# A hybrid decoder block on one core: four seven-product pairs in the embedding gate, differences stored later and written as one operation, attention steps in another order

## The chip, the cores and the metric

The kernel runs on one core of a Trainium2 chip. The metric is device time in microseconds of one execution; less is better. Times here are medians of runs, and the profile is of one execution of its own.

## The reference

One decoder layer on x of 256 tokens by 2048 channels, in float32. All matmuls below are with weights read from memory once.

```python
proj = x @ w_in                       # splits: gq gk gv gr glr fq fk fv ff ma mb
o    = gla_chunked(q, k, v, log_a)    # 4 heads, chunks of 64, then RMS norm and silu(gr)
y_gla = o @ w_branch_gla
of   = fox_attention(fq, fk, fv, log_f)   # 8 heads, softmax over 256, blocks of 128
y_fox = of @ w_branch_fox
x = layer_norm(ALPHA*x + (sigmoid(ma)*y_gla + sigmoid(mb)*y_fox) @ w_out)
g = causal_dwconv(x @ w_gate, conv_w, conv_b)     # width 3, 5632 channels
x = layer_norm(ALPHA*x + (gelu(g) * (x @ w_up)) @ w_down)
x = x + sigmoid(x @ w_ple_gate) * (p @ w_ple_proj)
```

## The kernel before

Weights arrive in units of 1 MB (`wu[u]`, 128 partitions by 2048). Each value is split in two parts, `hi` (rounded copy, made by ScalarE) and `lo` (the rest, made by VectorE, line 254), so that the product keeps its accuracy; TensorE multiplies hi by all columns and lo by those of the activations' high part. The plain route is `prep(u)`: SyncE loads two `raw` tiles, ACT copies them to `hi{u}_0`, `hi{u}_1`, DVE subtracts to `lo{u}_0`, `lo{u}_1`. `unit()` prepares three units ahead. There are five raw buffers and six of hi and of lo.

Stages follow one another: fox projections, attention and GLA; branch projections; out projection; layer norm; `gate_up` with 88 units (136 to 223: for n = 0 to 43 a gate unit `psg{n}` and an up unit `psu{n}`, so `psg40` is unit 216); the down projection; the embedding gate (`pg`).

A unit of gate_up is 16 matmuls of 512 columns (hi) and 16 of 256 (lo), in pairs; every 14th unit (`TURN`) has another order: six pairs, then the other lo's, then the other hi's. When PE ends it, ACT copies half to `tmp`, DVE adds the other half (`gp` or `up`, line 363), POOL copies two columns for the conv, DVE does the conv on `yc`, ACT the gelu, and DVE multiplies by `up`; the result goes to a tile hC, of which there are eleven, each for four n. For some pairs of n DVE also forms `sums` and `hs`, stored by POOL to `sd`.

Some pairs of K tiles in the later stages are done by seven products of 2x2 blocks instead of eight: 21 matmuls of 512 columns instead of 24. They need sums of activations (`s_sums`, `g_sums`) and differences of weight blocks. For the pairs listed in a table ending in `_T` the differences are made early: `park_gen` loads the unit into a `td` tile (SyncE, line 191), DVE makes four differences in place (line 172), POOL stores the tile to memory (line 185), and `prep_s` loads it again when its stage comes. In gate_up the generator is advanced by `pull(1, parks)`, once an n: one n loads, the next n parks. Tiles `td`, hC (the first ten) and the four tiles `x1T` of activations share one pool of 15 buffers of 8 KB a partition, "S8".

The order of ACT, DVE, POOL and mostly PE is set by a planner from the program's dependences and its own costs; SyncE's queue keeps program order, and each engine runs its queue in order. So a load that waits for a buffer holds up all loads behind it. `fox_gen` gives out the three steps of each attention head (logits, turn, values) between other matmuls.

Of the kernel before, what the change touches and what calls it, by code (L numbers as in the profile page):

```python
# [14 lines left out]
ALU = mybir.AluOpType  # L15
# [4 lines left out]
P = 128  # L20
# [52 lines left out]
WO_T = ((1, 2, 3, 4, 5), (1, 3, 5))  # L73
DN_T = ((3, 6, 9, 12, 15, 18), (3, 6, 9, 12, 15))
PG_ORDER = (tuple(range(8)), tuple(range(8)))
PG_S = ((), (2, 3, 4))
PG_T = ((), (2, 3, 4))
AFF1 = ((0, 2, 3), (0, 2))
AFF2 = ((0, 2), (0, 2))
LN_ORDER = (1, 0, 3, 2)  # L80
# [7 lines left out]
def tile_block(ctx: ExitStack, tc: tile.TileContext, wu, wfv, wpp, xT_in, x_in, pT_in, wlr,  # L88
               chan, gnorm, lng, ident_in, mask_in, cmask_in, out):
    nc = tc.nc  # L90
# [77 lines left out]
        return rhi.tile([P, 1088], F32R, tag="hi", name=f"hi{name}")[:, o:o + 1024]  # L168

    def differences(r0, r1, h, pinned=False):  # L170
        b12, b11, b22, b21 = r0[:, 0:512], r0[:, 512:1024], r1[:, 0:512], r1[:, 512:1024]
        sub = lambda o, a, b: nc.vector.tensor_tensor(o, a, b, ALU.subtract)  # L172
        if h == 0:
            i = sub(b11, b12, b11)
            if pinned:
                tc.keep_in_program_order(i)
            sub(b12, b12, b22)
        else:
            sub(b22, b22, b11)
            sub(b21, b21, b22)  # L180

    def park(w, i):
        for h in range(2):
# [14 lines left out]
    def prep_s(u):  # L198


        r0, r1 = [ring.tile([P, 1024], F32, tag="raw", bufs=5, name=f"raw{u}_{h}")
                  for h in range(2)]
        b12, b11, b22, b21 = r0[:, 0:512], r0[:, 512:1024], r1[:, 0:512], r1[:, 512:1024]
        rt = (r0, r1)
        if u in parked:
            nc.sync.dma_start(b11, wu[u, :, 512:1024])
            nc.sync.dma_start(r1, wu[u, :, 1024:2048])
            w = s8([P, 2048], name=f"td{u}")
            nc.sync.dma_start(w, td[parked[u]])
            rt = (w[:, 0:1024], w[:, 1024:2048])  # L210
        else:
            for h, r in enumerate((r0, r1)):
                nc.sync.dma_start(r, wu[u, :, h * 1024:(h + 1) * 1024])
        if dn0 <= u < dn0 + NF:
            nh = (u - dn0) // (NF // 2)
            pair = DN_ORDER[nh][(u - dn0) % (NF // 2)]
            i = DN_S[0].index(pair)
            if i % 2 == 0:
                two = s8([P, 8, 256], F32R, name=f"hS{nh}_{pair}")
                nc.sync.dma_start(two.bitcast(F32), sd[i // 2].rearrange(  # L220
                    "p (i n) -> p i n", i=8))
                hS[nh, pair], hS[nh, DN_S[0][i + 1]] = two[:, 0:4], two[:, 4:8]

        def split(src, name, e=slice(0, 1024)):
            hi = hi_tile(u, f"{u}_{name}")[:, e]
            lo = lo_tile(u, f"{u}_{name}")[:, e]
            copy(hi, src)
            nc.vector.tensor_tensor(lo, src, hi.bitcast(F32), ALU.subtract)  # L228
            return [(hi[:, o:o + 512], lo[:, o:o + 512]) for o in range(0, src.shape[1], 512)]

        x11, = split(b11, "b11", slice(512, 1024))
        x22, x21 = split(r1, "b2")
        if u not in parked:
            differences(r0, r1, 0)
        t3, t1_ = split(rt[0], "t13")
        if u not in parked:
            differences(r0, r1, 1)
        t2_, t4 = split(rt[1], "t24")
        ready[u] = [x11, x21, x22, t1_, t3, t2_, t4]
# [245 lines left out]
    for u in range(8):  # L485
        hi, lo = fvu[u]
        for j in range(2):
            kt = 2 * u + j
            a = xT[kt // 4][:, kt % 4, :]
# [6 lines left out]
            for t, i, c in seq:  # L496
                o, n = fch[c]
# [35 lines left out]
    for t in range(2):  # L533
        for c, (o, n) in enumerate(fch):
            n = min(n, 1024 - o)
# [75 lines left out]
    def fox_gen():  # L611


        lgs, sts, ptss = {}, {}, {}
        halves = ((256, 128), (0, 256))

        def logits(h):
            pl = mxtile(f"pl{h}")
            q, k = [fqk[h // 4][:, h % 4, i] for i in range(2)]
            for t, (o, n) in enumerate(halves):  # L620
                nc.tensor.matmul(pl[:, o:o + n], lhsT=q[:, t * P:t * P + P], rhs=k[:, 0:n],
                                 start=True, stop=True)
            lg = lgs[h] = t2("lg")[:, 0:384]
            for t, (o, n) in enumerate(halves):
                nc.vector.scalar_tensor_tensor(lg[:, o:o + n], pl[:, o:o + n],
                                               ct[:, t * FH + h:t * FH + h + 1],
                                               ncb[:, h * 256:h * 256 + n], ALU.add, ALU.add)
            nc.vector.tensor_tensor(lg[:, P:384], lg[:, P:384], cmask, ALU.add)
            st = sts[h] = sm.tile([P, 8], F32, tag="fst", name="fst")
            nc.vector.tensor_reduce(st[:, 0:1], lg[:, 256:384], AX.X, ALU.max, negate=True)  # L630
            nc.vector.tensor_reduce(st[:, 1:2], lg[:, 0:256], AX.X, ALU.max, negate=True)

        def softmax(h):
            lg, st = lgs[h], sts.pop(h)
            for t, (o, n) in enumerate(halves):
                nc.scalar.activation(lg[:, o:o + n], lg[:, o:o + n], AF.Exp,
                                     bias=st[:, t:t + 1], scale=1.0,
                                     accum_out=st[:, 2 + t:3 + t])
            nc.vector.reciprocal(st[:, 4:6], st[:, 2:4])
            for t, (o, n) in enumerate(halves):  # L640
                nc.vector.tensor_scalar(lg[:, o:o + n], lg[:, o:o + n], st[:, 4 + t:5 + t],
                                        None, ALU.mult)

        def turn(h):
            lg = lgs.pop(h)
            pt = mxtile(f"pt{h}")
            for i, d in enumerate((1, 2, 0)):
                nc.tensor.transpose(pt[:, d * P:d * P + P], lg[:, i * P:i * P + P], ident)
            pts = ptss[h] = t2("pts")[:, 0:384]
            copy(pts, pt[:, 0:384])  # L650

        def values(h):
            pts = ptss.pop(h)
            po = mmtile(f"po{h}")
            nc.tensor.matmul(po[:, 0:256], lhsT=fv[:, 0, h * P:h * P + P], rhs=pts[:, 0:256],
                             start=True, stop=False)
            nc.tensor.matmul(po[:, 128:256], lhsT=fv[:, 1, h * P:h * P + P],
                             rhs=pts[:, 256:384], start=False, stop=True)
            dst = ofT[h // 4][:, h % 4, :]
            copy(dst[:, 0:256], po[:, 0:256])  # L660
            nc.vector.tensor_tensor(dst[:, 256:512], po[:, 0:256],
                                    dst[:, 0:256].bitcast(F32), ALU.subtract)

        for i in range(FH + 2):
            for f, h in ((values, i - 2), (turn, i - 1), (logits, i)):
                if 0 <= h < FH:
                    f(h)
            yield
            if i < FH:
                softmax(i)  # L670
            yield
# [7 lines left out]
    for n in range(16):  # L679
        h, j = n // 2, n % 2  # L680
# [115 lines left out]
    for n in range(16):  # L796
        nm, dst, sc = (("q", gq, 1.0 / 16.0), ("k", gk, 1.0))[n // 2 % 2]
        h, c = n // 4, n % 2
# [274 lines left out]
    for nh in range(2):  # L1073
        def ev_r(t, c, ps, nh=nh):
# [3 lines left out]
            if 2 * nh + c == 0:  # L1078
# [3 lines left out]
               residual=False)  # L1082
# [71 lines left out]
    for n in range(PSM1, 32):  # L1154
        if n in (26, 28):
            i = n // 2 - 13
# [290 lines left out]
    for n in range(NF):  # L1447
# [18 lines left out]
        u = t1("up")  # L1466
# [4 lines left out]
        if pair in DN_S[0]:  # L1471
            if j == 0:
                yp = t2("yp").rearrange("p (k t) -> p k t", t=S)
            h = yp[:, j, :]
        else:
            h = y
# [4 lines left out]
        if pair in DN_S[0] and j == 1:  # L1481
            v = s_sums(yp)
            for i in range(2):
# [5 lines left out]
                o = k % 2 * 1024 + 512 * i  # L1489
                nc.gpsimd.dma_start(sd[k // 2, :, o:o + 512],  # L1490
                                    w.rearrange("p i n -> p (i n)").bitcast(F32))
        if n >= 4:
            pull(1)
        if n >= 4:
            pull(1, parks)


# [135 lines left out]
    def g_sums(pairs):  # L1633
        two = s8([P, 8, 256], F32R, name=f"gS{pairs[0]}")
        for i, pair in enumerate(pairs):
            o = two[:, 4 * i:4 * i + 4]
            a = x2T[pair // 2][:, pair % 2 * 2:pair % 2 * 2 + 2, :].bitcast(F32)
            y = t2("gy").rearrange("p (k t) -> p k t", t=S)
            nc.vector.tensor_tensor(y, a[:, :, 0:256], a[:, :, 256:512], ALU.add)
            v = s_sums(y)  # L1640
            copy(o[:, :, 0:P], v)
            nc.vector.tensor_tensor(o[:, :, P:256], v, o[:, :, 0:P].bitcast(F32), ALU.subtract)
            gS_[pair] = o
# [25 lines left out]

    def mid4():  # L1670
        mid3()
        g_sums(PG_S[1][:2])

    x_half("pg0", x2T, 16, lambda t, c, ps: put(ps, 0, t, c), pulls=2,
           begin=begin2, mid=(mid4, 4))

    s_half("pg", 1, PG_ORDER[1], PG_S[1], g_cl, g_st, lambda t, g: zg[:, t, g - 2, :], ev_g,
           3, {0: lambda: g_sums(PG_S[1][2:])}, residual=False, fine=pre_g)
    assert n_used[0] == NU, (n_used[0], NU)


# [23 lines left out]
def _sst(w, orders, ssets):  # L1705


    out = []
    for nh, (order, sset) in enumerate(zip(orders, ssets)):
        for n in order:  # L1710
            b = [[w[(2 * n + j) * P:(2 * n + j + 1) * P,
                    nh * 1024 + c * 512:nh * 1024 + c * 512 + 512] for c in range(2)]
                 for j in range(2)]
            out.append(np.concatenate([b[0][1], b[0][0], b[1][1], b[1][0]] if n in sset
                                      else b[0] + b[1], 1))
    return np.stack(out)

# [67 lines left out]
```

## Time and profile before

| | |
|---|---|
| median of 3 runs | 1638.0 us (1636.72 to 1638.08) |
| profiled execution | 1637.74 us; its span 1635.9 us |
| TensorE clock granted in it | 1.0 |
| PE busy | 1629.3 us |
| DVE, ACT, POOL busy | 1356.9, 909.5, 91.2 us |
| moved by DMA | 477.81 MB, 292 GB/s |

The span is what the profile covers; 1.8 us of the execution lie around it. Busy time of PE is that of overlapping matmuls; how long a matmul holds PE is read from the starts of the next ones, or from counts in a stretch of time. DMA times are from issue to landing.

### The profile page before, as it was taken

To read this page: it belongs to the slowest core of one execution; us is meant where nothing else is said; L and a number is where in the kernel's file an instruction comes from. 1 tells how busy PE (TensorE), PEld (TensorE's weight loads), DVE (VectorE), ACT (ScalarE), POOL (GpSimd) and SP (SyncE) were. 2 spreads that over 40 slices of the span, in tenths; PEclk is the share of its full clock that TensorE was granted. 3 is DMA by queue.
4 is the path that set the end of the run, shared out by engine and by line. 5 is a ranking of instruction groups with operands and counts; after the bars stand their busy time and mean duration, and the time that the engine had idled before them with its cause. 6 is when DMAs were issued, how large, how long until landed. Compare 5 with 4: busy or idle time off the path is not lost.

```text
span 1635.9 us, 23491 instructions
## 1 busy us (share of the span) xinstructions
PE 1629.3 (100%) x8422; PEld 1396.6 (85%) x8422; DVE 1356.9 (83%) x1964; ACT 909.5 (56%) x1277; POOL 91.2 (6%) x244
## 2 busy tenths in 40 slices
PE   9999999999999999999999999999999999999998
PEld 9988888888888888888898888888888888888887
DVE  7698899788989867878987888888887788988787
ACT  6655555456666653446574455555455456566554
POOL 0000000000000000000010111110111000000000
PEclk9999999999999999999999999999999999999999
DMA  8799899878888758889856898888776679899574
GB/s 325 283 370 345 292 390 353 293 262 299 308 322 326 253 189 320 304 317 393 299 181 198 321 347 322 292 310 312 282 252 221 204 273 339 307 355 344 166 260 156
DMA packets 114838, 477.81 MB, mean 292 GB/s; under 512 B 13032, under 2 KB 14320, under 8 KB 95136
## 3 DMA queue, kind: packets, MB, share of 16 engines
q1 hardware_dynamic: 105216, 417.57, 71.9%
q0 software_dynamic: 9504, 58.73, 9.0%
q8 instruction: 66, 1.08, 0.3%
q14 instruction: 52, 0.43, 0.1%
HBM read 417.53 MB, written 58.73 MB: 291 GB/s over the span
## 4 chain that ended last, share of the span: by engine, by line
PE 96%; DVE 2%; DMA 1%; ACT 1%; issue 0%; POOL 0%; SPq 0%; ACTq 0%; DVEq 0%; POOLq 0%
PE psm L1006 11%; PE dn L868 10%; PE psu L319 9%; PE psg L319 8%; PE psa L1006 5%; PE psu L324 4%; PE psg L324 4%; PE dn_p L868 4%; PE wo L868 3%; PE gr L868 3%; PE gv L868 3%; PE pg L380 3%; PE psb L1006 3%; PE fv L499 2%; PE gr_p L868 2%; PE gv_p L868 2%
## 5 line engine op out<-in xcount | busy, mean ns | idle before, releaser
L254 DVE TENSOR_TENSOR lo<-raw,hi 128x1024 fp32r<-128x1024 f32 x456 | 551.9, 1222 | 135.7 <-ACT hi L130 134.6
L130 ACT ACTIVATE hi<-raw 128x1024 fp32r<-128x1024 f32 x456 | 476.9, 1057 | 299.0 <-DMA raw<-in_wu_dram 68.4
L319 PE MATMUL psg<-x1T,hi 128*128 128x512 f32 x672 | 231.2, 390 | 0.0
L319 PE MATMUL psu<-x1T,hi 128*128 128x512 f32 x688 | 230.2, 390 | 0.0
L324 PE MATMUL psg<-x1T,lo 128*128 128x256 f32 x672 | 186.2, 277 | 0.6 <-DVE lo L254 0.6
L324 PE MATMUL psu<-x1T,lo 128*128 128x256 f32 x688 | 180.5, 277 | 0.0
L1006 PE MATMUL psm<-hi,xT 128*128 128x512 f32 x512 | 163.1, 393 | 0.0
L319 PEld LDWEIGHTS psu<-x1T,hi 128*128 128x128 f32 x688 | 128.7, 188 | 26.7
L319 PEld LDWEIGHTS psg<-x1T,hi 128*128 128x128 f32 x672 | 126.2, 188 | 26.4
L130 ACT ACTIVATE hi_b<-raw 128x512 fp32r<-128x512 f32 x112 | 93.1, 841 | 68.3 <-DMA raw<-in_wu_dram 16.4
L324 PEld LDWEIGHTS psg<-x1T,lo 128*128 128x128 f32 x672 | 126.1, 188 | 0.9 <-DVE lo L254 0.9
L324 PEld LDWEIGHTS psu<-x1T,lo 128*128 128x128 f32 x688 | 125.3, 188 | 0.6
L172 DVE TENSOR_TENSOR td<-td 128x512 f32<-128x512 f32 x172 | 118.3, 688 | 0.9
L228 DVE TENSOR_TENSOR lo_b<-raw,hi_b 128x512 fp32r<-128x512 f32 x112 | 105.3, 955 | 16.5 <-ACT hi_b L130 16.2
L1006 PEld LDWEIGHTS psm<-hi,xT 128*128 128x128 f32 x512 | 96.2, 188 | 19.6
L228 DVE TENSOR_TENSOR lo_t<-td,hi_t 128x1024 fp32r<-128x1024 f32 x86 | 101.8, 1222 | 12.5 <-ACT hi_t L130 11.7
L130 ACT ACTIVATE hi_t<-td 128x1024 fp32r<-128x1024 f32 x86 | 88.1, 1053 | 31.3 <-DMA td<-td 20.2
L1006 PE MATMUL psm<-lo,xT 128*128 128x512 f32 x256 | 99.9, 390 | 0.0
L868 PE MATMUL dn<-hi,hC 128*128 128x512 f32 x352 | 97.9, 390 | 0.0
L1006 PE MATMUL psa<-hi,oT 128*128 128x512 f32 x256 | 81.3, 392 | 0.0
L868 PEld LDWEIGHTS dn<-hi,hC 128*128 128x128 f32 x352 | 66.0, 188 | 13.6
L1006 PEld LDWEIGHTS psa<-hi,oT 128*128 128x128 f32 x256 | 48.1, 188 | 9.9
(414 smaller groups left out, 3129.4 us busy)
## 6 DMA issues: line engine op xcount, KB each, us to landing
raw<-in_wu_dram SPq DMA_DIRECT2D x525, 512.0 KB, 6.3
td<-in_wu_dram SPq DMA_DIRECT2D x43, 1024.0 KB, 8.7
td<-td POOLq DMA_DIRECT2D x43, 1024.0 KB, 6.7
td<-td SPq DMA_DIRECT2D x43, 1024.0 KB, 8.0
hS<-sd SPq DMA_DIRECT2D x11, 1024.0 KB, 8.9
raw<-in_wu_dram SPq DMA_DIRECT2D x43, 256.0 KB, 7.6
fvraw<-in_wfv_dram SPq DMA_DIRECT2D x13, 524.0 KB, 6.7
sd<-hs POOLq DMA_DIRECT2D x24, 256.0 KB, 5.8
```

Source lines behind the costliest of these rows:

```text
L130: return nc.scalar.activation(o, i, AF.Copy, bias=0.0, scale=scale)
L172: sub = lambda o, a, b: nc.vector.tensor_tensor(o, a, b, ALU.subtract)
L228: nc.vector.tensor_tensor(lo, src, hi.bitcast(F32), ALU.subtract)
L254: i = nc.vector.tensor_tensor(lo, raw, hi.bitcast(F32), ALU.subtract)
L319: nc.tensor.matmul(ps, lhsT=hi[i // 8][:, i % 8 * P:i % 8 * P + P], rhs=act[kts[i] // 4][:, kts[i] % 4, :], start=first and i == 0, stop=l ...
L324: nc.tensor.matmul(ps[:, 256:512], lhsT=lo[i // 8][:, i % 8 * P:i % 8 * P + P], rhs=act[kts[i] // 4][:, kts[i] % 4, 0:256], start=False, s ...
L380: nc.tensor.matmul(bs[j][:, 0:m], lhsT=x, rhs=v[:, o:o + m], start=first and i == 0, stop=last and i == 2)
L499: nc.tensor.matmul(fbk[t][c][:, 0:n], lhsT=x, rhs=w[:, o:o + n], start=kt == 0 and i == 0, stop=kt == 15 and i == 2)
L868: nc.tensor.matmul(ps[:, e], lhsT=x, rhs=w, start=k == 1, stop=k == total.get(id(ps), 3 * ns))
L1006: nc.tensor.matmul(ps[t], lhsT=x, rhs=v, start=first and i == 0 and j == 0, stop=last and i == 3 and j == 2)
```

## The change

Four edits. The gate's second half treats pairs 1 to 4 by seven products instead of 2 to 4, all parked (44 parked units instead of 43), and forms the sums of both couples in the middle of the first half. In a parked tile the first two differences become one operation of 128x1024, with block b12 read twice; for this the host writes the first two blocks of such a unit in the other order. In the attention the steps of one turn go turn, logits, values instead of values, turn, logits. In gate_up the generator of parked units is advanced from n = 10 instead of n = 4.

```diff
-PG_S = ((), (2, 3, 4))
-PG_T = ((), (2, 3, 4))
+PG_S = ((), (1, 2, 3, 4))
+PG_T = ((), (1, 2, 3, 4))
...
     def differences(r0, r1, h, pinned=False):
...
+            two = r0.rearrange("p (i n) -> p i n", i=2)
+            if r0.tensor is r1.tensor:
+                four = bass.AP(tensor=r0.tensor, offset=r0.offset,
+                               ap=[r0.ap[0], [1024, 2], [1, 512]])
+                i = nc.vector.tensor_tensor(two, two[:, 1:2].broadcast_to([P, 2, 512]), four,
+                                            ALU.subtract)
...
-            for f, h in ((values, i - 2), (turn, i - 1), (logits, i)):
+            for f, h in ((turn, i - 1), (logits, i), (values, i - 2)):
...
-        if n >= 4:
+        if n >= 10:
             pull(1, parks)
...
     def mid4():
         mid3()
-        g_sums(PG_S[1][:2])
+        for i in (0, 2):
+            g_sums(PG_S[1][i:i + 2])
...
-           3, {0: lambda: g_sums(PG_S[1][2:])}, residual=False, fine=pre_g)
+           3, {}, residual=False, fine=pre_g)
...
-            out.append(np.concatenate([b[0][1], b[0][0], b[1][1], b[1][0]] if n in sset
+            out.append(np.concatenate([b[0][0], b[0][1], b[1][1], b[1][0]] if n in sset
```

How the change moves instructions late in gate_up. First SyncE's queue at the loads of units 215 to 217, before; a `raw` has its unit's number.

```order
L250 DMA raw214_1_12310<-in_wu_dram 128x1024
L250 DMA raw215_0_12361<-in_wu_dram 128x1024
L250 DMA raw215_1_12367<-in_wu_dram 128x1024
L250 DMA raw216_0_12413<-in_wu_dram 128x1024
L250 DMA raw216_1_12419<-in_wu_dram 128x1024
L250 DMA raw217_0_12470<-in_wu_dram 128x1024
```

SyncE at the same place now:

```order
L256 DMA raw214_1_12267<-in_wu_dram 128x1024
L256 DMA raw215_0_12318<-in_wu_dram 128x1024
L256 DMA raw215_1_12324<-in_wu_dram 128x1024
L197 DMA td43_12370<-in_wu_dram 128x2048
L256 DMA raw216_0_12372<-in_wu_dram 128x1024
L256 DMA raw216_1_12378<-in_wu_dram 128x1024
L256 DMA raw217_0_12429<-in_wu_dram 128x1024
```

The load of the last parked tile, td43, stands ahead of unit 216's raw loads; before, no parked tile is loaded this late.

VectorE around lo216_0, before; `psg38` is unit 212, `psu38` 213, `psu39` 215, and the `up` or `gp` line is the first DVE step after PE has ended that unit.

```order
L254 TENSOR_TENSOR lo215_1_12371<-raw215_1_12367,hi215_1_12369 128x1024
L363 TENSOR_TENSOR gp38_12349<-psg38_12316,tmp_12351 128x256
L1458 TENSOR_SCALAR yc_12356<-gp38_12349,chn_116 128x256
L1463 SCALAR_TENSOR_TENSOR yc_12356<-gp38_12349,chn_116,yc_12356 128x256 x2
L254 TENSOR_TENSOR lo216_0_12417<-raw216_0_12413,hi216_0_12415 128x1024
L254 TENSOR_TENSOR lo216_1_12423<-raw216_1_12419,hi216_1_12421 128x1024
L363 TENSOR_TENSOR up_12406<-psu38_12373,tmp_12407 128x256
```

VectorE around lo216_0 now:

```order
L1464 TENSOR_SCALAR yc_12424<-gp39_12417,chn_116 128x256
L1469 SCALAR_TENSOR_TENSOR yc_12424<-gp39_12417,chn_116,yc_12424 128x256 x2
L369 TENSOR_TENSOR up_12474<-psu39_12441,tmp_12475 128x256
L1483 TENSOR_TENSOR yc_12424<-yc_12424,up_12474 128x256
L260 TENSOR_TENSOR lo216_0_12376<-raw216_0_12372,hi216_0_12374 128x1024
L1486 TENSOR_TENSOR hC9_12128<-yc_12424,hC9_12128 128x256
L177 TENSOR_TENSOR td43_12370<-td43_12370 128x1024
L260 TENSOR_TENSOR lo216_1_12382<-raw216_1_12378,hi216_1_12380 128x1024
```

Before, lo216_0 stands behind the first steps on unit 212, three units back; now it stands behind those on unit 215, and its second half behind the differences of td43.

GpSimd (POOL) at the last stores from gate_up, now; `gp{n}` is the conv's buffer of n, `hs` the sums that are stored.

```order
L1458 MEMSET gp40_12530 128x2
L1496 DMA sd_111<-hs_12249 128x512
L1496 DMA sd_111<-hs_12253 128x512
L1458 MEMSET gp41_12640 128x2
L1458 MEMSET gp42_12749 128x2
L1458 MEMSET gp43_12858 128x2
L1462 COPY gp38_12306<-gp38_12306 128x1 x2
L191 DMA td_110<-td42_12133 128x2048
```

Before, the last store of a parked tile in gate_up, that of td42, stands ahead of gp35; now td42's stands behind the last memset, and td43's behind it.

More of the change, by code (lines that the diff above doesn't have):

```diff
@@ L170, in differences @@
     def differences(r0, r1, h, pinned=False):
-        b12, b11, b22, b21 = r0[:, 0:512], r0[:, 512:1024], r1[:, 0:512], r1[:, 512:1024]
-        sub = lambda o, a, b: nc.vector.tensor_tensor(o, a, b, ALU.subtract)
+        b22, b21 = r1[:, 0:512], r1[:, 512:1024]
         if h == 0:
[L174 to L177, printed above, removed]
-        else:
-            sub(b22, b22, b11)
-            sub(b21, b21, b22)
+            two = r0.rearrange("p (i n) -> p i n", i=2)
[4 more added lines that the diff above has]
+                                            ALU.subtract)
+                if pinned:
+                    tc.keep_in_program_order(i)
+                return
+            nc.vector.tensor_tensor(two[:, 0], two[:, 1], two[:, 0], ALU.subtract)
+            nc.vector.tensor_tensor(two[:, 1], two[:, 1], b22, ALU.subtract)
+        else:
+            nc.vector.tensor_tensor(b22, b22, r0[:, 0:512], ALU.subtract)
+            nc.vector.tensor_tensor(b21, b21, b22, ALU.subtract)
     def park(w, i):
@@ L202, in prep_s @@
                   for h in range(2)]
-        b12, b11, b22, b21 = r0[:, 0:512], r0[:, 512:1024], r1[:, 0:512], r1[:, 512:1024]
+        b11 = r0[:, 0:512]
         rt = (r0, r1)
         if u in parked:
-            nc.sync.dma_start(b11, wu[u, :, 512:1024])
+            nc.sync.dma_start(b11, wu[u, :, 0:512])
             nc.sync.dma_start(r1, wu[u, :, 1024:2048])
@@ L229, in split @@
             return [(hi[:, o:o + 512], lo[:, o:o + 512]) for o in range(0, src.shape[1], 512)]
-        x11, = split(b11, "b11", slice(512, 1024))
+        x11, = split(b11, "b11", slice(0, 512))
         x22, x21 = split(r1, "b2")
@@ L234, in prep_s @@
             differences(r0, r1, 0)
-        t3, t1_ = split(rt[0], "t13")
+        t1_, t3 = split(rt[0], "t13")
         if u not in parked:
```

## The prediction

> **What bounds the kernel now.** I read the page first, its busy table and its chain.
>
> ```profile
> PE 1629.3 (100%) x8422; PEld 1396.6 (85%) x8422; DVE 1356.9 (83%) x1964; ACT 909.5 (56%) x1277; POOL 91.2 (6%) x244
> PE 96%; DVE 2%; DMA 1%; ACT 1%; issue 0%; POOL 0%; SPq 0%; ACTq 0%; DVEq 0%; POOLq 0%
> ```
>
> PE is busy in 1629.3 of 1635.9 us and carries 96% of the chain. A change can gain by issuing fewer matmuls, by removing one of PE's few waits, or by letting matmuls follow each other faster. It loses wherever PE has to wait for new reasons. So I asked next for PE's own waits.
>
> ```profile
> PE warm_ps L140 <- DVE warm L137: 1.2, 1, 1.2
> PE psg L324 <- DVE lo L254: 0.6, 1, 0.6
> ```
>
> The first is the start. The second is the only wait of the long stages: once, 0.6 us, in gate_up. DVE's timeline puts it at 939 us, unit 156 (psg10).
>
> ```profile
> 935.01 0.69 DVE L1293 TENSOR_TENSOR z<-z,lnb 128x512 f32<-128x512 f32 x1
> 935.62 0.42 DVE L363 TENSOR_TENSOR gp<-psg,tmp 128x256 f32<-128x256 f32 x1
> 936.59 1.07 DVE L1463 SCALAR_TENSOR_TENSOR yc<-gp,chn,yc 128x256 f32<-128x256 f32 x2
> 939.15 3.50 DVE L254 TENSOR_TENSOR lo<-raw,hi 128x1024 fp32r<-128x1024 f32 x3 [1.50 <-ACT hi L130]
> ```
>
> DVE had done the differences of a parked unit and a layer-norm step late, so the conv, the gelu and the hi copy behind them on ACT came late too. The wait has an after-effect, seen in counts of matmuls in equal stretches. Here are two in gate_up, then two in the attention.
>
> ```profile
> 944.00:1000.00 56.00, 56.00 (x325) 1.00 0.91 335
> 1008.00:1064.00 56.00, 56.00 (x332) 1.00 0.83 308
> 79.00:90.00 11.00, 11.00 (x67) 1.00 0.99 363
> 91.00:102.00 11.00, 11.00 (x65) 1.00 1.01 408
> 1594.76:1600.20 5.44, 5.44 (x26) 1.00 1.02 419
> 1600.20:1604.96 4.76, 4.76 (x23) 1.00 0.63 222
> ```
>
> PE never idles in either gate_up stretch and the granted clock is 1.00 in both, yet after the wait it issues 2.1% fewer matmuls, until unit 167 (written in another order) restores the pace. So there are two paces of the same work. The last two rows are the embedding gate's second half: an ordinary pair in 5.44 us, a pair with seven products in 4.76.
>
> **The change part by part.** *Pair 1 by seven products.* It has 21 matmuls instead of 24, and 5.44 − 4.76 = **−0.68 us** on PE. It costs one more parked unit (a 1 MB load, DVE differences, a store, a reload). Its lo's come from a stored difference, like those of the pairs behind it, whose PE time shows no wait, and the sums of the second couple come earlier than they are needed. I cost them at nothing; their cover is PE's own 5.44 us a pair. If it fails, at most one lo is late.
>
> *Two differences as one operation.*
>
> ```profile
> L172 DVE TENSOR_TENSOR td<-td 128x512 f32<-128x512 f32 x172 | 118.3, 688 | 0.9
> L254 DVE TENSOR_TENSOR lo<-raw,hi 128x1024 fp32r<-128x1024 f32 x456 | 551.9, 1222 | 135.7 <-ACT hi L130 134.6
> ```
>
> Two of 0.69 become one of the size of a lo, 1.22: 0.15 us less, 44 times, 6.7 us of DVE. DVE is 17% idle and not on the chain, so: nothing, except where DVE is late.
>
> *Attention ends on values.* The same three steps of each head go between the same matmuls, but the value products are last. The pace alternates from one stretch to the next there (67 against 65 matmuls in 11 us). Which step leaves which pace no row says. If every stretch became fast I work out 0.9 us less from four slow ones of 11 us at 2.1%; if all fast ones became slow, about 0.7 more. I take 0. In the chunked attention behind it, kq stands four short DVE operations earlier in the new order:
>
> ```profile
> 370.42 0.39 PE L868 MATMUL gv<-hi,xT 128*128 128x512 f32 x1
> 370.91 0.71 PE L762 MATMUL pa<-kq 128*128 128x128 f32 x4
> ```
>
> These starts are 0.49 apart where 0.23 is the rule (5.44/24), which I count as gone: **−0.26 us**.
>
> *Parking from n = 10 instead of n = 4.* The wait at 939 us goes, since no parked work has reached DVE by then: −0.6, and the slow pace behind it, 2.1% of the 64 us up to unit 167, −1.3: together **−1.9 us**. But as many parked units (one more, in fact) now run six n later, up to n = 39, when the ten hC tiles and four x1T tiles have taken 14 of the 15 large buffers. So the load of td43 must wait until td42 has been stored. SP is a queue in program order, and behind that load stand both raw loads of unit 216 (psg40). In DVE's order lo216_0 stands behind the combination of psu39, that is of unit 215, the unit directly before; ACT's hi216_0 stands behind tmp of psu39. PE must then wait, whenever the data come. In the trace of before lo's lie at worst one unit further ahead, as here at unit 180:
>
> ```profile
> 1066.92 0.39 ACT L130 ACTIVATE tmp<-psg 128x256 f32<-128x256 f32 x1 [0.21 <-PE psg L324]
> 1067.20 1.05 ACT L130 ACTIVATE hi<-raw 128x1024 fp32r<-128x1024 f32 x1
> 1069.30 1.22 DVE L254 TENSOR_TENSOR lo<-raw,hi 128x1024 fp32r<-128x1024 f32 x1
> 1072.69 0.38 ACT L130 ACTIVATE tmp<-psu 128x256 f32<-128x256 f32 x1 [0.90 <-PE psu L324]
> ```
>
> PE ended unit 178 at 1066.9 and unit 179 at 1072.7; the lo of unit 180 was ready at 1070.5, and PE did not wait. In the new order unit 216 has no such unit in between, so it waits for tmp, hi and lo: 0.39 + 1.05 + 1.22 = 2.7 us. That is the lower bound. The raws may come later still, so I follow the transfers, with time zero where PE ends unit 211 (psu37):
>
> ```profile
> L363 DVE TENSOR_TENSOR up<-psu,tmp 128x256 f32<-128x256 f32 x28 | 11.8, 420 | 3.1 <-ACT tmp L130 3.1
> L1486 DVE TENSOR_TENSOR hs<-sums,hs 128x256 fp32r<-128x256 f32 x16 | 6.3, 421 | 1.3 <-ACT hs L130 1.3
> L824 DVE TENSOR_TENSOR sums<-yp 128x128 f32<-128x128 f32 x16 | 4.7, 291 | 0.4
> L1456 POOL COPY gp<-gp 128x1 f32<-128x1 f32 x58 | 17.4, 361 | 181.7 <-DVE gp L363 181.7
> td<-td POOLq DMA_DIRECT2D x1, 1024.0 KB, 4.4
> sd<-hs POOLq DMA_DIRECT2D x2, 256.0 KB, 4.4
> DMA to landing us min/median/max: 3.7/4.8/6.0
> 20.00:30.00 10.00, 10.00 (x65) 10.00 (x64) 9.45 (x10) 8.37 (x10) 0.00 (x0) 1.00 1.03 403
> ```
>
> The single 4.4s are from a stretch of gate_up (1056 to 1075 us) in which SP had stopped issuing, the third row from the end is of the raw loads at 1235 to 1275 us, and the last shows what the engines move at most, 403 GB/s. DVE works through up, the product, four lo's, hC, four sums and two hs: 0.4 (tmp) + 4 x 0.42 + 0.42 + 4 x 1.22 + 4 x 0.29 = 8.5. The hs store takes 4.4: 12.9. POOL's memset of gp43 takes the buffer that this store frees, and two copies of 0.36 follow it, all ahead of the store of td42: 13.7 (td42's differences are done at about 12). That store, 4.4: 18.1. Then SP issues td43's load (0.4) and raw216_0, which lands 3.7 later, plus 2.6 for the 1 MB ahead of it at 403 GB/s: 24.8. Then hi and lo: 27.1. PE reaches unit 216 after four units of 5.44 (16 x 512 and 16 x 256 columns, as many as an ordinary pair's 24 x 512): 21.8. The wait is 27.1 − 21.8 = **+5.3 us**. I take this and not the order's 2.7, because each link is a measured landing. With the page's median landing for such stores it is longer:
>
> ```profile
> td<-td POOLq DMA_DIRECT2D x43, 1024.0 KB, 6.7
> ```
>
> This makes 7.6, and with hs stores and raws as slow 8 to 9. Unit 212 stands in the same way behind td42's load, which waits for td41's store: 2.3 (to the end of td41's differences, behind unit 208) + 4.4 + 6.7 + 2.3 = 15.7 after the end of unit 208, against three units, 16.3. With slower landings it is a wait of up to 1.5; I take **+0.3**. Unit 216's second lo stands behind the 1.22 of td43's difference: about 0.1, within that. A wait may leave the slow pace, 0.12 us a unit, until unit 223: 0 to 1.2, I take **+0.5**.
>
> The sum: −0.68 − 0.26 − 1.9 + 5.3 + 0.3 + 0.5 = +3.3. On the profiled execution's 1637.74 that is 1641.0; the median of the runs, 1638.0, lies 0.3 above that execution, so +3.0 against it, 0.18%.
>
> **A rule weighed.** The trace's start shows what a cold PE costs.
>
> ```profile
> L140 PE MATMUL warm_ps<-warm 128*128 128x512 bf16 x8 | 3.6, 631 | 1.2 <-DVE warm L137 1.2
> ```
>
> Eight matmuls of 512 columns take 3.6 us, 0.45 each against 0.23 later. The wait of 0.6 us did not bring this back. Whether one of 5 us does, no row here can tell. If it does, about 3.6 us of work at half pace cost 1.8 us: rival A.
> [...]
>
> **The rivals.** *A, slower: the clock falls in the wait at unit 216, or the stores land at the page's median.* Place: units 216 and 217. Price: 1.8, or 2.3 (7.6 for 5.3); time 1642.8 to 1643.3, both together 1645. [...] For it: POOL's stores land in 4.4 to 8 elsewhere. Against it: SP stands still here, so the engines are quiet. Chance 0.31.
> *B, the order alone.* The raws land before PE ends unit 215; the wait is 2.7, with nothing at 212. 1641.0 − 2.6 − 0.3 = 1638.1. For it: raw loads land 3.7 to 6.0 after issue when nothing stands ahead. Against it: the queue on SP. Chance 0.17.
> *C, faster: the late parks cost nothing.* If td43 finds a free buffer and DVE catches up, only the gains stay: 1637.74 − 2.8 = 1634.9, or 1634.0 with a fast attention. Against it stands the order of DVE and ACT. Chance 0.07.
> That the change does not do what it says is possible for its gain at 939 us alone: if another wait arises there, A's times hold.
>
> **How the numbers follow.** My forecast (chance 0.45) is 1641.0, with 1639.5 to 1642.5 from the attention's pace (−0.9 to +0.7) and the pace after the wait (−0.5 to +0.7). The range 1637.0 to 1644.5 takes in B's and most of A's and leaves out C. What a measurement of this kernel can tell is about 0.2%, 3.3 us: faster means below 1634.7, slower above 1641.3. Faster is most of C and the edge of B: 0.07. Within 0.2%: about three fifths of the forecast, B and a little of the rest: 0.47. Slower: two fifths of the forecast, and A: 0.46.
>
> **What would show it.** Right: no wait of PE at 939 us; in gate_up a wait of PE for hi or lo at psg40 of about 5 us, with the issue of td43's load some 18 us after unit 211's end, and no raw load issued for several us ahead of it; 21 matmuls in the gate's pair 1; about 6.7 us less of DVE for the differences. Wrong: PE waits under 3 us in the whole of gate_up (B or C), or raw216 is issued before td42's store lands. A shows as matmuls of 0.45 us behind the wait. If the time is below 1636, a term that I priced at nothing, the pace above all, was large.

## The result, and the profile after

| | before | changed |
|---|---|---|
| median | 1637.34 us (5 runs) | 1646.74 us (5 runs, 1645.37 to 1647.67) |
| ratio of the two | | 1.0057, 95% interval 1.0044 to 1.0069 |
| span of the profiled execution | 1635.9 us | 1645.0 us |

The changed kernel is slower by 9.4 us. The forecast was 1641.0, the range ended at 1644.5. First the busy table and the chain of the page of the changed kernel, then PE's own waits (total, times, longest).

```profile
PE 1633.0 (99%) x8419; PEld 1398.3 (85%) x8419; DVE 1357.8 (83%) x1932; ACT 914.6 (56%) x1280; POOL 95.1 (6%) x245
PE 93%; DVE 3%; DMA 2%; issue 1%; ACT 1%; POOL 0%; SPq 0%; DVEq 0%; ACTq 0%
PE psg L325 <- ACT hi L130: 3.7, 2, 2.2
PE psg L330 <- DVE lo L260: 1.5, 2, 0.8
PE warm_ps L140 <- DVE warm L137: 1.2, 1, 1.2
PE gr_p L874 <- DVE lo_t L234: 0.7, 1, 0.7
PE pg L874 <- DVE lo L260: 0.4, 1, 0.4
```

PE issues three matmuls less and is busy 3.7 us longer: some of its matmuls ran slower. Where before had one wait in the long stages, there are now four places. PE's timeline has the two in gate_up, ahead of psg38 (unit 212) and psg40 (216); between the two idle stretches of each stands one matmul.

```profile
1246.12 0.28 PE L330 MATMUL psu<-x1T,lo 128*128 128x256 f32 x1
1248.55 0.50 PE L325 MATMUL psg<-x1T,hi 128*128 128x512 f32 x1 [2.15 <-ACT hi L130]
1249.81 0.58 PE L330 MATMUL psg<-x1T,lo 128*128 128x256 f32 x1 [0.76 <-DVE lo L260]
...
1272.87 0.28 PE L330 MATMUL psu<-x1T,lo 128*128 128x256 f32 x1
1274.74 0.51 PE L325 MATMUL psg<-x1T,hi 128*128 128x512 f32 x1 [1.59 <-ACT hi L130]
1276.01 0.39 PE L330 MATMUL psg<-x1T,lo 128*128 128x256 f32 x1 [0.76 <-DVE lo L260]
```

The windows view of PE around them (us, busy with the number of matmuls, granted clock, DMA share, GB/s), three windows of 3.41 us for each place, laid so that they meet where the granted clock changes:

```profile
1246.26:1249.67 3.41, 0.63 (x3) 1.00 1.02 417
1249.67:1253.08 3.41, 3.27 (x10) 0.50 0.87 318
1253.08:1256.49 3.41, 3.41 (x21) 1.00 0.80 263
1273.57:1276.98 3.41, 1.48 (x7) 1.00 0.89 358
1276.98:1280.39 3.41, 3.41 (x12) 0.50 0.64 205
1280.39:1283.80 3.41, 3.41 (x21) 1.00 0.80 265
```

At each place the granted clock is 0.50 for 3.41 us: 10 and 12 matmuls where there are 21 at the full clock. The two falls lie 27.31 us apart, eight times 3.413, and the first lies 364 times 3.413 us behind the start of the trace's clock record. So in this trace both falls lie on one grid of 3.41 us, and its stretches are called steps here: each fall comes at the end of the step that holds most of the idle time, which at psg40 is 1 us after PE has begun again (1276.98 against 1276.01).

Lining up the starts of the same matmuls in the two traces tells where the 9.1 us of span arose: +0.2 by the time the fox projections run (in the other traces −0.2 to +0.6), +0.3 in the attention, −0.3 in and behind the chunked attention, +1.0 at gr_p and +0.6 at wo_p (seven-product pairs of the projection to gr and of the out projection), −2.1 in gate_up between 939 us and 1007 us, **+5.0 at psg38** (3.35 of wait, 1.65 of slow matmuls), **+4.5 at psg40** (2.8 and 1.73), −0.7 by the gate's three matmuls, +0.65 at a late lo near the gate's end.

What made the raws late is in the queues. Before, SP issued raw loads there without a break:

```profile
1236.29 48.40 SPq L250 DMA_DIRECT2D raw<-in_wu_dram  x19
```

Now SP's row, then POOL's stores of parked tiles, then ACT and DVE at the two units:

```profile
1239.79 0.33 SPq L197 DMA_DIRECT2D td<-in_wu_dram  x1
1240.21 13.50 SPq L256 DMA_DIRECT2D raw<-in_wu_dram  x8
1265.43 0.33 SPq L197 DMA_DIRECT2D td<-in_wu_dram  x1
1265.86 23.16 SPq L256 DMA_DIRECT2D raw<-in_wu_dram  x13
1235.62 0.54 POOL L191 DMA_DIRECT2D td<-td  x1 [0.26 <-DVE td L186]
1261.29 0.54 POOL L191 DMA_DIRECT2D td<-td  x1
1247.44 1.06 ACT L130 ACTIVATE hi<-raw 128x1024 fp32r<-128x1024 f32 x1 [3.46 <-DMA raw<-in_wu_dram]
1248.53 1.23 DVE L260 TENSOR_TENSOR lo<-raw,hi 128x1024 fp32r<-128x1024 f32 x1 [5.07 <-ACT hi L130]
1273.25 0.38 ACT L130 ACTIVATE tmp<-psu 128x256 f32<-128x256 f32 x1 [2.58 <-PE psu L330]
1273.63 1.06 ACT L130 ACTIVATE hi<-raw 128x1024 fp32r<-128x1024 f32 x1
1274.72 1.23 DVE L260 TENSOR_TENSOR lo<-raw,hi 128x1024 fp32r<-128x1024 f32 x1 [0.18 <-ACT hi L130]
```

td41's store is issued at 1235.62, td42's load 4.2 us later, when it has landed, and unit 212's raws right behind that load; 4.1 us lie between td42's store and td43's load. SP issues no load from 1253.7 to 1265.4. At psg38 ACT waits for the raw itself. At psg40 hi follows tmp of the unit before, and two bounds meet: the raw landed at 1273.61, and that tmp was done at 1273.63.

### The profile page after: what moved, and what is told of

The parts are those of the page before. It is cut to its first block, busy times and chain, and to the rows that moved or that the text cites. A ratio compares the mean times of both kernels' runs of the same rounds, so it can differ in the third digit from the quotient of the medians.

```text
span 1645.0 us, 23465 instructions
## 1 busy us (share of the span) xinstructions
PE 1633.0 (99%) x8419; PEld 1398.3 (85%) x8419; DVE 1357.8 (83%) x1932; ACT 914.6 (56%) x1280; POOL 95.1 (6%) x245
## 4 chain that ended last, share of the span: by engine, by line
PE 93%; DVE 3%; DMA 2%; issue 1%; ACT 1%; POOL 0%; SPq 0%; DVEq 0%; ACTq 0%
PE psm L1012 11%; PE dn L874 10%; PE psg L325 8%; PE psu L325 8%; PE psa L1012 5%; PE psg L330 4%; PE psu L330 4%; PE dn_p L874 4%; PE wo L874 3%; PE gv L874 3%; PE fv L505 3%; PE pg L386 3%; PE psb L1012 3%; PE gr L874 2%; PE gv_p L874 2%; PE psk L325 2%
## 5 line engine op out<-in xcount | busy, mean ns | idle before, releaser
L874 PEld LDWEIGHTS dn<-hi,hC 128*128 128x128 f32 x352 | 66.0, 188 | 13.7
L1470 ACT ACTIVATE yc<-yc 128x256 f32<-128x256 f32 x44 | 18.3, 417 | 69.5 <-DVE yc L1469 69.4
```

The costliest lines, as they stand in the source:

```text
L874: nc.tensor.matmul(ps[:, e], lhsT=x, rhs=w, start=k == 1, stop=k == total.get(id(ps), 3 * ns))
L1470: nc.scalar.activation(y, y, AF.Gelu_apprx_tanh, bias=0.0, scale=1.0)
```

## The experiments

**The edits one by one**, each put alone into the kernel before. Later parking:

```diff
-        if n >= 4:
+        if n >= 10:
             pull(1, parks)
```

> The kernel before with the later parking alone (n >= 10), 43 parked units. Theory (the late parked tiles share one buffer, and SP's queue holds the raw loads behind them): only one load, td42's at n = 36, now finds the pool full, because there is no 44th unit; so one wait of PE of about 3 us at psg38 and about 1.7 us of half-rate matmuls behind it, none at psg40, and the wait at 939 us with its slow pace is gone (-2.1): +2 to +3 us, 1640. Rival (late parking as such makes DVE late, whatever the buffers): waits at psg38 and later of 8 to 9 us as in the changed kernel, +7 us, 1644.

Measured 1.0018 (1.0008 to 1.0027), 1640.23 us against 1637.38. One place with waits, psg38, with the half clock behind it, and none at psg40:

```profile
PE psg L319 <- ACT hi L130: 1.5, 1, 1.5
PE psg L324 <- DVE lo L254: 0.8, 1, 0.8
1248.00:1250.50 2.50, 2.50 (x9) 0.50 1.01 341
```

The two traces lined up: −2.1 between 939 and 1007 us, +4.2 at psg38. The second late wait goes with the load of td43, the 44th parked unit, which another edit brings: the edits together cost more than the sum of them. The later parking and the fourth pair alone, with both loads on SP, were not run.

The fourth pair alone:

```diff
-PG_S = ((), (2, 3, 4))
-PG_T = ((), (2, 3, 4))
+PG_S = ((), (1, 2, 3, 4))
+PG_T = ((), (1, 2, 3, 4))
```

> The kernel before with the fourth seven-product pair alone, parking from n = 4. Theory: three matmuls less, -0.68, and a wait of some 0.5 to 0.65 us near the end of the gate that gives it back: 0 +-0.5 us; the 44th unit is parked at n = 32 and 33 and costs nothing. Rival (the extra unit itself costs the 4.5 us at psg40): +4 us.

0.9993 (0.9984 to 1.0002). The trace shows −0.68 in the gate and +0.52 at a late lo near its end. The 44th unit does no harm when parked early.

The differences as one operation, alone (with the host's order of the blocks):

```diff
-            i = sub(b11, b12, b11)
...
-            sub(b12, b12, b22)
+                i = nc.vector.tensor_tensor(two, two[:, 1:2].broadcast_to([P, 2, 512]), four,
+                                            ALU.subtract)
```

> The kernel before with the two differences as one operation alone. Theory: nothing in gate_up, the wait at 939 us stays (0.6 us or a little less); the new wait of 0.9 us at gr_p and 0.6 us at wo_p come from this edit, since both stages use parked differences: +1 to +1.6 us. Rival (those two come from the attention's order): 0 us here.

1.0010 (1.0000 to 1.0019). +1.0 us at wo_p, as expected; nothing at gr_p, so half of the expectation failed. Nor did gate_up stay as it was: the trace has a wait of 0.8 us for a lo at 986 us, which before does not have. ACT's waits in the stretch around wo_p, of before and of this kernel:

```profile
ACT hi_t L130 <- DMA td<-td: 1.4, 1, 1.4
```

```profile
ACT hi_t L130 <- DMA td<-td: 2.9, 2, 1.7
```

The reloads of parked tiles land later. All seven profiled kernels with this edit lose 0.5 to 1.1 us at wo_p; of the five others one loses 0.37 and four less than 0.15. At gr_p four of the seven lose 0.5 to 1.0, none of the five does. Why reloads are later with this edit was not found.

The attention's order alone:

```diff
-            for f, h in ((values, i - 2), (turn, i - 1), (logits, i)):
+            for f, h in ((turn, i - 1), (logits, i), (values, i - 2)):
```

> The kernel before with the attention's steps ending on values alone. Theory: +0.25 us in the attention and -0.26 in the chunked attention: 0 us, no new wait at gr_p. Rival: gr_p's wait of 0.9 us and wo_p's 0.6 appear here, +1 to +1.5 us.

1.0002 (0.9993 to 1.0012): +0.3 in the attention, as in the changed kernel. The −0.26 in the chunked attention did not come: 0.15 of it shows in all seven traces with the single operation and in no other, and the rest, 0.1 at 488 us, in every trace but that of before. One thing was not expected: this trace has the −2.1 in gate_up, though it parks from n = 4. PE has no wait at 939 us, and its pace behind is the fast one:

```profile
944.00:1000.00 56.00, 56.00 (x332) 1.00 0.91 341
```

DVE made the lo's of that place at nearly the same time as before (from 938.86 us, against 939.15), but PE came 0.7 us later. So that wait is a close one, and PE can miss it with the parking as it was.

**Where the buffer runs out.** The changed kernel with parking from n = 4 and from n = 6:

> The changed kernel with its late parking undone (n >= 4, 44 units, last load at n = 32). Theory (the loss is the one buffer at n = 36 and 38): no wait at psg38 or psg40, -9.5; the wait at 939 us may come back (+0.6 to +2.1); the rest of the change stays with gr_p's wait of 0.9, wo_p's 0.6 to 1.0 and the gate's 0: 1638 to 1640 us, +1 to +2 over before. Rival (the differences as one operation or the 44th unit make the late waits): above 1642.

> The changed kernel with parking from n = 6: the 44 units' last load is at n = 34, before hC9 takes its buffer at n = 36. Theory: no wait at psg38 and psg40, as with n >= 4: 1637 to 1639.5 us. Rival (every unit parked late costs something, in proportion): half way, 1641 to 1643 us.

1.0015 (1.0006 to 1.0025) and 1.0007 (0.9998 to 1.0017), 1639.28 and 1638.55 us against 1636.94. Neither has a wait of PE at psg38 or psg40; park6 has one of 1.4 us in two parts at 986 us. The loss at psg38 and psg40 is no matter of how late all units are parked; it comes with the loads at n = 36 and 38. park4 still lies 2.3 us above the kernel before: its trace loses 0.5 at gr_p and 1.1 at wo_p, keeps most of the wait and pace behind 939 us, and has the slow pace a second time between 1010 and 1200 us (0.8).

**SP's queue.** The buffer stays scarce, but the two late loads are given out by POOL:

```diff
-            nc.sync.dma_start(w, wu[u])
+            (nc.gpsimd if parked[u] >= 42 else nc.sync).dma_start(w, wu[u])
```

> The changed kernel, with the loads of td42 and td43 alone given out by POOL's queue instead of SP's. The buffer is as scarce as before, but the raw loads of units 212 and 216 no longer stand behind these loads. Theory (SP's queue passes the wait for the buffer on to the raws): no wait at psg38 and psg40, no half-rate matmuls: -9.5 us, 1637 to 1638 us. Rival (the scarce buffer delays PE by another way, through the differences on DVE or the conv's copies on POOL): waits of 3 us and more stay, 1641 to 1646 us.

0.9994 (0.9985 to 1.0004), 1637.03 us. SP's row and POOL's:

```profile
1238.56 35.40 SPq L256 DMA_DIRECT2D raw<-in_wu_dram  x16
1259.29 0.54 POOL L191 DMA_DIRECT2D td<-td  x1 [0.66 <-DMA sd<-hs]
1266.24 0.54 POOL L197 DMA_DIRECT2D td<-in_wu_dram  x1 [6.30 <-DMA td<-td]
```

POOL now stands 6.3 us for td42's store, and PE does not wait for it (DVE does, 0.77 us, for a copy behind it); the raw loads run on, and PE has no wait in gate_up. Not the buffer but the queue that waits for it cost 9.5 us. One caution: the planner set the order anew for this kernel. The first hi of unit 216 stands ahead of psu39's tmp again (PE begins psg40 at 1268.43, that tmp begins at 1269.53), so at psg40 the late raw and the late place in the order went together, and no run parts them.

**The clock.** The changed kernel with extra matmuls into an unused tile, ahead of psg38 and psg40:

```diff
+        if name in ("psg38", "psg40"):
+            fill = mxtile(f"fill{name}")
+            for i in range(12):
+                tc.keep_in_program_order(nc.tensor.matmul(
+                    fill, lhsT=x1T[0][:, 0, 0:P], rhs=x1T[0][:, 0, :], start=True, stop=True))
```

> The changed kernel with 12 extra matmuls of 512 columns (2.7 us, into an unused tile) on PE ahead of psg38 and of psg40. Theory: they lie in the waits of 3.3 and 2.8 us, and keep PE at its full rate, so the half-rate matmuls behind (0.43 us instead of 0.23; 1.65 and 1.73 us in all) go: -3.4 us, 1643.3 us, with waits of under 1 us left. Rival (the slow matmuls behind the waits are late lo's, not the clock): matmuls still 0.43 us apart there, 1646 to 1647 us; if the waits are not idle at all, +5 us.

1.0052 (1.0037 to 1.0067), 1646.02 us. The half clock is gone at both places; the windows behind the waits:

```profile
1250.20:1252.70 2.50, 2.50 (x15) 1.00 0.98 347
1276.60:1279.10 2.50, 2.50 (x15) 1.00 1.02 411
```

At psg38 the loss fell from 5.0 to 3.4 us by lining up, as expected. At psg40 it fell only from 4.5 to 4.3: PE came there earlier, ended unit 215 at 1272.2 and then waited for the raw, which landed at 1274.1 in this run. Here hi stands ahead of psu39's tmp, so the raw alone holds PE:

```profile
1274.19 1.06 ACT L130 ACTIVATE hi<-raw 128x1024 fp32r<-128x1024 f32 x1 [4.46 <-DMA raw<-in_wu_dram]
```

Of the expected −3.4, 1.6 came at psg38; the other half came back as waiting, and by the medians little is left of it (this trace also loses 0.9 us to the slow pace between 1010 and 1200 us). With 4 instead of 12:

> The changed kernel with 4 extra matmuls of 512 columns (0.9 us) instead of 12 ahead of psg38 and psg40. The idle time left is about 2.4 us at psg38 and 1.9 us at psg40, each in two parts around one matmul. Theory (a few us of near-idle PE bring the half rate): at psg38 matmuls still 0.43 us apart for some 3 us, at psg40 perhaps not; time as the changed kernel's, 1645 to 1647 us. Rival (only an idle stretch of over 3 us does it): full rate behind both, 1643 us.

1.0055 (1.0038 to 1.0072). PE's timeline and windows:

```profile
1248.34 0.51 PE L325 MATMUL psg<-x1T,hi 128*128 128x512 f32 x1 [1.62 <-ACT hi L130]
1249.60 0.39 PE L330 MATMUL psg<-x1T,lo 128*128 128x256 f32 x1 [0.76 <-DVE lo L260]
1246.61:1250.02 3.41, 1.04 (x4) 1.00 1.03 412
1250.02:1253.43 3.41, 3.41 (x12) 0.50 0.74 267
...
1274.51 0.51 PE L325 MATMUL psg<-x1T,hi 128*128 128x512 f32 x1 [0.55 <-ACT hi L130]
1275.78 0.38 PE L330 MATMUL psg<-x1T,lo 128*128 128x256 f32 x1 [0.76 <-DVE lo L260]
1273.91:1277.33 3.42, 2.11 (x11) 1.00 1.00 386
1277.33:1280.74 3.41, 3.41 (x22) 1.00 0.79 250
```

Behind 1.62 + 0.76 = 2.4 us idle in two parts the clock was 0.50, behind 0.55 + 0.76 = 1.3 it was 1.00. The windows are again steps of 3.41 us: the clock fell behind the one in which PE was busy 1.04 us, and not behind the one with 2.11. The fall did not come in every run of a kernel, either: in four of the ten runs of only_park10 the mean granted clock is 1.000, where one step at 0.50 would make it 0.999. Whether the wait was shorter in these runs, or lay otherwise in the steps, no trace shows.

**Better versions.** The kernel before with the fourth pair and parking from n = 6:

> The kernel before with four seven-product pairs and parking from n = 6, without the single operation and without the attention's order: no late load finds the pool full (last at n = 34), the gate's three matmuls are saved and partly given back by a late lo (-0.2). Theory: the wait at 939 us goes with its pace (-2.1): 1635 us, faster than both. Rival (that wait comes from the layer norm's work on DVE alone, whatever is parked): 1637 us.

0.9996 (0.9987 to 1.0006). The wait at 939 us went, the slow pace did not (325 matmuls from 944 to 1000 us, as before), so the gain was 0.7 and not 2.1. With parking from n = 10 and the two late loads on POOL:

> The kernel before with four seven-product pairs, parking from n = 10 and the two late loads on POOL's queue; two operations for the differences, the attention in its old order. Theory: the wait at 939 us and its pace gone (-2.1), three matmuls less (-0.68) with 0.5 given back, no late waits: 1635 us, faster than before by 1.5 to 2.3 us. Rival (the wait at 939 us is no longer there in most runs of before, or POOL's queue is held up): 1637 us or more.

> The same kernel as pg4_park10_pool (the kernel before with four seven-product pairs, parking from n = 10, the two late loads on POOL's queue), timed in more rounds, to see whether it is faster than before. From its first ratio, 0.9991: 0.9990 +-0.0006, 1.6 us less than before, an interval below 1. Rival (no difference that can be told): the interval holds 1.

0.9991 (0.9982 to 1.0001) and 0.9994 (0.9985 to 1.0003). The trace has the expected −2.1 and −0.68, and gives 1.1 back at the late lo in the gate. Both medians lie 1.1 to 1.8 us below before's; both intervals hold 1, so it is not shown to be faster than the kernel before. Against the changed kernel it is 11 us faster.

## Why the prediction was wrong, point by point

*The mechanism held.* One buffer left, td43's load waiting for td42's store, the raws of unit 216 behind it on SP, hi and lo behind the unit directly before: all of it is in the trace, and late_pool shows that the queue is the cause. The forecast had the right place and the right direction of the loss. Its size was off by the clock (3.4 us for nothing), by three small losses (2.25 for nothing) and by two waits in gate_up that were sized wrongly, one too small and one too large.

*The clock, rival A, was the step that failed.* "Whether one of 5 us does, no row here can tell. If it does, about 3.6 us of work at half pace cost 1.8 us." Waits of 3.35 and 2.8 us did, at two places: 1.65 + 1.73 = 3.4 us. It is the largest term that the sum lacks; less these 3.4 us the median would be 1643.3, inside the range. I gave A a chance of 0.31, and one place. By the forecast's own sum PE stood idle 4.1 us before the first matmul of unit 216 (hi done at 24.8 + 1.05, PE there at 21.8). The longest idle stretch in each wait behind which the clock fell was 1.49 (only_park10) to 2.15 us (psg38), so, by what these runs show, the term belonged in the sum. The clock fell behind steps of 3.41 us in which PE was busy 0.63 and 1.48 us (the changed kernel), 1.64 (only_park10) and 1.04 (filled4), and stayed at 1.00 behind steps with 2.03 (park6), 2.11 (filled4) and 2.41 (filled). In the four with a fall PE was idle 1.8 to 2.8 us.

*Unit 212: +0.3 forecast, 3.35 measured.* I let td41's store go out 2.3 us behind unit 208. It went out 5.6 us behind: PE ended that unit at 1230.0, the store was issued at 1235.62. DVE was still at unit 207's up, sums, hC and hs until 1232.3, with a lo between. The store then took 4.1, against the 4.4 that I had, and from td42's load to the raw's landing it was 7.6 instead of 6.7. I had counted the work of DVE in full for unit 216, and not for unit 212.

*Unit 216: +5.3 forecast, 2.8 measured.* The raw landed 27.2 us after unit 211's end, against 24.8 in my sum: td42's store went out at 14.9 instead of 13.7, and from its landing to the raw's it was 8.2 us instead of 6.7. (The 403 GB/s in that sum are not the most that the engines move: the prediction's own rows have 408 and 419.) But PE itself came 5.0 later, held at psg38, so that the data were there when tmp was done (raw landed 1273.61, hi began 1273.63). What was left is the order's bound, 2.7. Two waits in one chain share their lateness: together they were 6.15 us, against 5.6 forecast. That the totals lie so near is partly luck, as neither wait had its forecast size.

*What I priced at nothing.* gr_p +1.0, wo_p +0.6, the gate's late lo +0.65: 2.25 together. That "at most one lo is late" was true, and it cost all that the three matmuls gain. The edit with the one DVE operation saves 7 us of DVE as worked out (0.688 twice against 1.217), and that was worth nothing; the reloads behind it came later.

*What held.* −2.1 in gate_up against −1.9, −0.68 in the gate, +0.3 in the attention within the bounds. But the reasons held in part only. The −2.1 is in all seven traces with parking from n = 10, and also in that of only_values, with parking from n = 4; so the one trace of before may overstate what the later parking gains, and the times do not show the gain (pg4_park10_pool). I took the slow pace to be an after-effect of the wait at 939 us. In only_pg4 that wait is there (0.8 us) and the pace is full, 331 matmuls from 944 to 1000 us; in pg4_park6 there is no wait and the pace is slow, 325. What sets the pace stays open. The −0.26 in the chunked attention came in size, by luck: not from the attention's order, as forecast, but 0.15 with the single operation and 0.1 in every trace but before's. The +0.5 for a slow pace behind the wait did not come: the changed kernel's lag on before stays at 9.2 us from psg40 to the gate.

The sum with the measured terms: −2.1 − 0.7 − 0.3 + 0.2 + 0.3 + 1.0 + 0.6 + 0.65 + 6.15 + 3.4 = +9.2, against 9.1 between the spans.

## What to carry to other kernels

When work is moved later, look at who shares its buffers there, and at what stands behind its loads on the queue that will wait: here SP's queue, in program order, handed one scarce buffer on to the raw loads of units 212 and 216 (1646.74 us with the two late loads on SP, 1637.03 with them on POOL). A load that may wait belongs on a queue whose followers have slack: POOL stood 6.3 us for td42's store, and PE had no wait in gate_up. Price a long wait of PE with its clock, at each place: here idle time of 2.25 to 2.9 us in two parts was followed by a granted clock of 0.50 in the four traced waits, and 1.3 us was not (filled4, psg40). Follow a chain from its first link with the engine's backlog, since a first wait moves the second: PE came to psg40 5.0 us later here, and waited 2.8 us there instead of the 5.3 forecast.

## What the runs showed of the hardware

In the changed kernel PE's granted clock was 0.50 twice in gate_up, for 3.41 us each time. The two falls lie 27.31 us apart, eight times 3.413, and the first comes 364 times 3.413 us after the trace's clock record begins; steps of 3.41 us are counted from there. In traces without such a fall they are counted from that beginning too, which is an assumption: no fall marks them there. The clock was 0.50 for one step behind each step in which PE was busy 0.63 to 1.64 us, four of four, though idle stretches of 1.5 to 2.15 and 0.76 us had a matmul between them; behind steps with 2.03 to 2.41 us of busy time it stayed at 1.00, three of three. Whether the place of a wait in the steps counts beside its length was not shown; no run tried the same wait at another place. At psg40 the fall came 1 us after work had begun again: the first pairs started 0.34 us apart, those behind the fall 0.64. With 12 extra matmuls (2.7 us) into an unused tile ahead of psg38 and psg40 the clock was 1.00 behind both (filled). The same 32 matmuls a unit ran at two paces 2% apart (325 and 331 or 332 matmuls in 56 us), at a granted clock of 1.00, with a wait ahead (325 before, 331 in only_pg4) or without (325 in pg4_park6, 332 in only_values).
